# A batched matrix product with the second operand transposed: the first load in two transfers, one wait handed from TensorE to VectorE, the closing waits handed from GpSimd to SyncE

## The chip, the cores and the metric

The kernel runs on one core of a Trainium2 chip. The metric is the device time of one execution in microseconds (us); lower is better. The profile is one execution taken by the hardware profiler. Engines are named as there: PE is TensorE's matmul, PEld its weight load, DVE is VectorE, ACT is ScalarE, POOL is GpSimd, SP is SyncE; a "q" behind a name means the engine's sequencer. "L93" is line 93 of the kernel.

## The reference

```python
batch, m, k, n = 16, 512, 512, 512
a: (batch, m, k) float32      b: (batch, n, k) float32
return np.matmul(a, b.transpose(0, 2, 1)).astype(np.float32)
```

Sixteen products of 512x512 matrices are wanted, each of a with the transpose of b. The inputs are 2 x 16.8 MB, the output 16.8 MB.

## The kernel before

The 16 matrices are worked in 8 pairs. For each pair, u, one load brings two matrices of a (2 MB), another two matrices of b. All loads are issued by SP on one DMA queue. Each of the 128 partitions holds 8 rows of 512 float32 values, 16 KB in all; there are seven such load buffers, ld0 to ld6, and 16 loads, so that the eighth load waits until its buffer has been read. The first two loads (of a and b for the first pair) are cut into halves of 1 MB along the rows of a partition, lines L93 and L96, each half with a semaphore of its own: `s_ld` for the first, `s_second` for the second half.

DVE casts what has landed to bf16, in two halves (L116, L121), into `ha` and `hb`. PE transposes 128x128 blocks with an identity matrix (L185) into the PSUM tile `tp`; ACT copies the transposed a to `ta` (L137), DVE the transposed b to `tb` (L126). Then PE multiplies (L199, 32 matmuls of 128x512 per pair) into `ps`, and ACT copies each result to an output buffer (L153), of which there are seven, ob0 to ob6. An output of 1 MB is stored by one DMA. ACT issues the first (L163), SP the other 15 (L105).

Everything stands in one critical section, in which the engines are ordered by semaphores that are written out by hand, not by the framework. SP's order of loads and stores is written out as a string, `ORDER`, of 16 L and 15 S: seven loads, two of them in halves, are issued at the start without any wait; after these, loads and stores alternate by the string, each behind its own wait (a load for a free buffer, a store for a finished output). PE's work is a loop over the pairs on PE's sequencer (`Fori`, L172); the other engines' code is unrolled.

At the start POOL makes the identity `ident` in two steps (L67, L69), which raise `s_set` to 2. PE waits for that in front of its loop (L171). The wait in the loop's first step is `take(s_c, 1)`, for DVE's cast of the whole of `ha`.

At the end the last seven stores must have landed. A second critical section holds seven waits on POOL for this, one for each store semaphore (L212 to L214). Between the two sections the framework puts a meeting of the engines (L40): SP signals, every other engine answers, SP signals again. After the second section it puts a closing barrier over all engines (L240). SP stands in this closing part and waits for POOL to leave its section.

A wait on an engine is, in the built program, an instruction of the engine's sequencer, or is joined to the one that follows. In the trace POOL's seven waits, joined with those of the framework, are six instructions in a row.

Of the kernel before, what the change touches and what calls it, by code (L numbers as in the profile page):

```python
# [10 lines left out]
def kernel(  # L11
# [6 lines left out]
    nc = tc.nc  # L18
    P = 128
    batch, M, K = a.shape  # L20
    _, N, _ = b.shape
    J = M // P
# [5 lines left out]
    NL = 7  # L28
    NO = 7
# [4 lines left out]
    def sbuf(name, shape, dtype):  # L34
        return ctx.enter_context(nc.sbuf_tensor(name, shape, dtype))

    def sem(name):
        return tc.alloc_semaphore(name)

    with tc.tile_critical(no_gpsimd_drain=True):  # L40
        ident = sbuf("ident", [P, P], bf16)
        ld = [sbuf(f"ld{i}", [P, 2 * J, K], f32) for i in range(NL)]
# [8 lines left out]
        s_set = sem("s_set")  # L51
        s_ld = [sem(f"s_ld{i}") for i in range(NL)]
        s_second = [sem(f"s_second{i}") for i in range(2)]
        s_st = [sem(f"s_st{i}") for i in range(NO)]
# [23 lines left out]
        n_ld, n_st = 0, 1  # L78
        for what in ORDER:
            if what == "L":  # L80
                u, slot = n_ld // 2, n_ld % NL
                src = (a if n_ld % 2 == 0 else b)[2 * u:2 * u + 2].rearrange(
                    "e (p j) k -> (e p) j k", j=2 * J
                )
                if n_ld >= NL:

                    v = (n_ld - NL) // 2
                    if (n_ld - NL) % 2 == 0:
                        nc.sync.wait_ge(s_half, 2 * v + 2)
                    else:  # L90
                        nc.sync.wait_ge(s_tb, KO * v + 1)
                if n_ld < 2:
                    nc.sync.dma_start(  # L93
                        ld[slot][:, :J, :], src[:, :J, :]
                    ).then_inc(s_ld[slot], 16)
                    nc.sync.dma_start(  # L96
                        ld[slot][:, J:, :], src[:, J:, :]
                    ).then_inc(s_second[slot], 16)
                else:
                    nc.sync.dma_start(ld[slot][:], src).then_inc(s_ld[slot], 16)  # L100
                n_ld += 1
            else:
                slot = n_st % NO
                nc.sync.wait_ge(s_out, n_st + 1)
                nc.sync.dma_start(  # L105
                    out[n_st].rearrange("(p j) n -> p j n", j=J), ob[slot][:]
                ).then_inc(s_st[slot], 16)
                n_st += 1

        for u in range(pairs):
            for x, (h, s_c) in enumerate(((ha, s_ca), (hb, s_cb))):
                n = 2 * u + x
                nc.vector.wait_ge(s_ld[n % NL], 16 * (n // NL + 1))
                nc.vector.tensor_copy(  # L116
                    out=h[:, :J, :], in_=ld[n % NL][:, :J, :]
                ).then_inc(s_half, 1)
                if n < 2:
                    nc.vector.wait_ge(s_second[n], 16)  # L120
                nc.vector.tensor_copy(  # L121
                    out=h[:, J:, :], in_=ld[n % NL][:, J:, :]
                ).then_inc(s_c, 1)
            for ko in range(KO):
                nc.vector.wait_ge(s_tb, KO * u + ko + 1)
                nc.vector.tensor_copy(  # L126
                    out=tb[:, ko, :],
                    in_=tp[:, (2 * ko + 1) % 4].rearrange("k j p -> k (j p)"),
                ).then_inc(s_eb, 1)
# [38 lines left out]
        def take(s, n):  # L168
            nc.tensor.wait_ge(s, n).then_inc(s, -n)  # L169

        nc.tensor.wait_ge(s_set, 2)  # L171
        with nc.Fori(  # L172
            0, pairs, engines=[nc.tensor.engine], head_slot={nc.tensor.engine: 24}
        ):
# [33 lines left out]
                    t.then_inc(s_mm, 1)  # L208

    with tc.tile_critical(no_gpsimd_drain=True):  # L212
        for n in range(batch - NO, batch):
            nc.gpsimd.wait_ge(s_st[n % NO], 16 * (n // NO + 1))  # L214


# [28 lines left out]
```

## Time and profile before

| | us |
|---|---|
| median of 4 runs | 127.39 |
| lowest and highest run | 127.12 and 127.88 |
| the profiled execution, its whole time | 127.28 |
| span of the profile, first to last instruction | 125.5 |
| busy: PE, PEld | 89.7, 56.5 |
| busy: ACT, DVE, POOL | 70.7, 59.2, 0.7 |
| first load issued | 0.94 |
| first cast (L116) starts | 6.12 |
| first transposes (L185) start on PE | 11.08 |
| last matmul ends, last copy of ACT (L153) starts | 115.16, 115.19 |
| last store issued | 115.80 |

The whole time is 1.78 us longer than the span; that part lies before the first and after the last instruction of the profile. A DMA's time is not that of its issue: an issue on SP takes 0.33 to 0.75 us of SP's time, and the data land later, by 16 DMA engines that the transfer is spread over. A landing is the moment at which one of these engines raises the transfer's semaphore, so a transfer of this kernel has 16 landings, and the last one releases who waits. The page's busy shares are averages over the span; the DMA row and the GB/s row in its slices say what the DMA engines do at the same time.

### The profile page before, as it was taken

What the parts mean: (1) busy time and instruction counts of PE and PEld (TensorE: products, weight loads), DVE (VectorE), ACT (ScalarE), POOL (GpSimd) and SP (SyncE); (2) the same over time, 40 slices, a digit from 0 to 9 for tenths busy, and PEclk for the clock granted to TensorE, in tenths of its full rate; (3) what the DMA queues carried; (4) which work ended last, traced back from release to release, by engine and by line L of the source; (5) the groups of instructions that cost most, each with busy time, mean ns of one, the idle gap of its engine ahead of it and who ended that gap; (6) DMA issues with size and microseconds to landing.
All of it is one profiled execution on the core that took longest, in us unless ns stands there. A gap on an engine that the chain in (4) does not pass through costs nothing. (4 is left out here: it accounts for less than half of the span.)

```text
span 125.5 us, 1959 instructions
## 1 busy us (share of the span) xinstructions
PE 89.7 (71%) x768; PEld 56.5 (45%) x768; DVE 59.2 (47%) x64; ACT 70.7 (56%) x129; POOL 0.7 (1%) x6
## 2 busy tenths in 40 slices
PE   0003089799699969996999699879586999697000
PEld 0002088347544854494459346734383449342000
DVE  0035525962793386549906970780666476200000
ACT  4001226468946875795669467946755679566000
POOL 2000000000000000000000000000000000000000
PEclk9999999999999999999999999999999999999965
DMA  4999999999999999999999999999999999999960
GB/s 86 394 426 436 428 444 433 423 418 410 389 428 415 444 399 428 441 433 428 410 439 423 413 460 402 405 441 389 462 428 423 413 423 433 420 423 426 439 269 8
DMA packets 4899, 50.37 MB, mean 401 GB/s; under 512 B 544, under 2 KB 544, under 8 KB 544
## 3 DMA queue, kind: packets, MB, share of 16 engines
q1 hardware_dynamic: 4752, 49.29, 93.8%
q10 hardware_dynamic: 144, 1.05, 2.0%
q8 instruction: 1, 0.02, 0.0%
q14 instruction: 2, 0.02, 0.0%
HBM read 33.55 MB, written 16.78 MB: 401 GB/s over the span
## 5 line engine op out<-in xcount | busy, mean ns | idle before, releaser
L199 PE MATMUL ps<-tb,ta 128*128 128x512 bf16 x256 | 56.5, 379 | 8.4 <-PEq L169 8.4
L153 ACT COPY ob<-ps 128x512 f32<-128x512 f32 x64 | 37.5, 586 | 26.4 <-PE ps L199 26.4
L137 ACT COPY ta<-tp 128x512 bf16<-128x512 bf16 x64 | 32.6, 625 | 17.8 <-PE tp L185 17.8
L199 PEld LDWEIGHTS ps<-tb,ta 128*128 128x128 bf16 x256 | 24.4, 97 | 37.9 <-issue 9.5
L126 DVE COPY tb<-tp 128x1024 bf16<-128x1024 bf16 x32 | 22.1, 691 | 28.4 <-PE tp L185 28.4
L185 PE MATMUL tp<-ident,ha 128*128 128x128 bf16 x256 | 21.2, 230 | 11.1 <-PEq L169 11.1
L185 PE MATMUL tp<-ident,hb 128*128 128x128 bf16 x256 | 20.8, 228 | 6.0 <-PEq L169 6.0
L185 PEld LDWEIGHTS tp<-ident,ha 128*128 128x128 bf16 x256 | 17.1, 104 | 13.7 <-issue 11.1
L185 PEld LDWEIGHTS tp<-ident,hb 128*128 128x128 bf16 x256 | 16.7, 102 | 6.5 <-issue 6.5
L116 DVE CAST hb<-ld 128x2048 bf16<-128x2048 f32 x8 | 9.8, 1224 | 9.7 <-DMA ld<-in_b_dram 9.7
L116 DVE CAST ha<-ld 128x2048 bf16<-128x2048 f32 x8 | 9.8, 1219 | 6.9 <-DMA ld<-in_a_dram 6.9
L121 DVE CAST ha<-ld 128x2048 bf16<-128x2048 f32 x8 | 9.8, 1221 | 2.4 <-DMA ld<-in_a_dram 2.4
L121 DVE CAST hb<-ld 128x2048 bf16<-128x2048 f32 x8 | 9.8, 1221 | 1.3 <-DMA ld<-in_b_dram 1.3
L137 ACT ACT_TABLE_LOAD x1 | 1.3, 1283 | 0.9 <-SPq L40 0.9
L69 POOL TENSOR_SCALAR_AFFINE_SELECT ident<-ident 128x128 bf16<-128x128 bf16 x1 | 0.3, 292 | 0.2 <-POOL ident L67 0.2
L67 POOL MEMSET ident<- 128x128 bf16 x1 | 0.2, 204 | 0.5 <-SPq L40 0.5
L229 POOL MEMSET const-bfloat16-1.0<- 128x1 bf16 x1 | 0.1, 101 | 0.0
L229 POOL MEMSET const-uint8-127<- 128x1 uint8 x1 | 0.1, 101 | 0.0
L229 POOL MEMSET const-float32-0.0<- 128x1 f32 x1 | 0.1, 98 | 0.2 <-issue 0.2
L229 POOL MEMSET const-float32-1.0<- 128x1 f32 x1 | 0.1, 98 | 0.0
## 6 DMA issues: line engine op xcount, KB each, us to landing
out_dram<-ob SPq DMA_DIRECT2D x15, 1024.0 KB, 25.6
ld<-in_a_dram SPq DMA_DIRECT2D x7, 2048.0 KB, 30.3
ld<-in_b_dram SPq DMA_DIRECT2D x7, 2048.0 KB, 31.5
ld<-in_a_dram SPq DMA_DIRECT2D x2, 1024.0 KB, 6.7
ld<-in_b_dram SPq DMA_DIRECT2D x2, 1024.0 KB, 11.3
out_dram<-ob ACTq DMA_DIRECT2D x1, 1024.0 KB, 12.6
```

The costliest lines, as they stand in the source:

```text
L67: nc.gpsimd.memset(ident[:], 0.0).then_inc(s_set, 1)
L69: nc.gpsimd.affine_select(out=ident[:], in_=ident[:], compare_op=mybir.AluOpType.not_equal, fill=1.0, base=0, pattern=[[-1, P]], channel_m ...
L116: nc.vector.tensor_copy(out=h[:, :J, :], in_=ld[n % NL][:, :J, :]).then_inc(s_half, 1)
L121: nc.vector.tensor_copy(out=h[:, J:, :], in_=ld[n % NL][:, J:, :]).then_inc(s_c, 1)
L126: nc.vector.tensor_copy(out=tb[:, ko, :], in_=tp[:, (2 * ko + 1) % 4].rearrange("k j p -> k (j p)"),).then_inc(s_eb, 1)
L137: c = nc.scalar.copy(out=ta[:, ko, e * J * P:(e + 1) * J * P].rearrange("k (j p h) -> k j p h", j=J, h=2), in_=tp[:, (2 * ko) % 4, :, e * ...
L153: c = nc.scalar.copy(out=ob[i % NO][:, j, :].rearrange("m (p j) -> m p j", j=2 * J), in_=ps[:, j, :].rearrange("m (j p) -> m p j", j=2 * J),)
L185: t = nc.tensor.transpose(tp[:, (2 * ko + x) % 4, j, :], h[:, j, ko * P:(ko + 1) * P], ident[:],)
L199: t = nc.tensor.matmul(ps[:, j, :], ta[:, ko, (e * J + j) * P:(e * J + j + 1) * P], tb[:, ko, :].rearrange("k (j p) -> k j p", j=2 * J)[:, ...
L229: nc = _bacc.Bacc("TRN2", target_bir_lowering=False, num_devices=1)
```

## The change

Four things change.

- The first half of the first load is issued as two transfers, of partitions 0 to 31 and of partitions 32 to 127, onto the same semaphore. DVE's waits on that semaphore count 16 more from there on. The halves behind it are issued as before, one place later.
- PE no longer waits for the identity in front of its loop.
- DVE waits for it instead, before its first cast. PE's first work waits for that cast.
- SP waits, at the end of the first section, for six of the last seven stores. The second section holds one wait, on SP, for the last store; POOL has none there.

The arithmetic and all other transfers stay.

```diff
-                if n_ld < 2:
+                if n_ld == 0:
+                    for p in (slice(0, 32), slice(32, P)):
+                        nc.sync.dma_start(
+                            ld[slot][p, :J, :], src[p, :J, :]
+                        ).then_inc(s_ld[slot], 16)
+                elif n_ld == 1:
                     nc.sync.dma_start(
                         ld[slot][:, :J, :], src[:, :J, :]
                     ).then_inc(s_ld[slot], 16)
+                if n_ld < 2:
                     nc.sync.dma_start(
                         ld[slot][:, J:, :], src[:, J:, :]
                     ).then_inc(s_second[slot], 16)
...
+        for n in range(batch - NO, batch - 1):
+            nc.sync.wait_ge(s_st[n % NO], 16 * (n // NO + 1))
...
+        nc.vector.wait_ge(s_set, 2)
         for u in range(pairs):
             for x, (h, s_c) in enumerate(((ha, s_ca), (hb, s_cb))):
                 n = 2 * u + x
-                nc.vector.wait_ge(s_ld[n % NL], 16 * (n // NL + 1))
+                nc.vector.wait_ge(
+                    s_ld[n % NL], 16 * (n // NL + 1 + (1 if n % NL == 0 else 0))
+                )
...
-        nc.tensor.wait_ge(s_set, 2)
         with nc.Fori(
...
     with tc.tile_critical(no_gpsimd_drain=True):
-        for n in range(batch - NO, batch):
-            nc.gpsimd.wait_ge(s_st[n % NO], 16 * (n // NO + 1))
+        nc.sync.wait_ge(s_st[(batch - 1) % NO], 16 * ((batch - 1) // NO + 1))
```

In the built program the order of the work on PE, DVE and ACT is the same as before. SP issues one transfer more, and POOL's instructions after the identity are those of the meeting and of the closing barrier alone.

## The prediction

> **What bounds the kernel now.** I read the page's slices first, then the queues, then the windows in stretches of 10 us, then the start and the end. The slices say that the DMA engines never rest between start and end, and the queue line says that one queue does it:
>
> ```profile
> DMA  4999999999999999999999999999999999999960
> GB/s 86 394 426 436 428 444 433 423 418 410 389 428 415 444 399 428 441 433 428 410 439 423 413 460 402 405 441 389 462 428 423 413 423 433 420 423 426 439 269 8
> ...
> q1 hardware_dynamic: 4752, 49.29, 93.8%
> ```
>
> The windows (columns: stretch, its length, busy time of PE, PEld, DVE, ACT, POOL, granted clock, DMA share, GB/s) say it per stretch:
>
> ```profile
> 0.00:10.00 10.00, 0.00 (x0) 0.00 (x0) 1.52 (x2) 1.28 (x1) 0.70 (x6) 1.00 0.80 309
> 10.00:20.00 10.00, 4.96 (x46) 4.75 (x47) 4.77 (x5) 2.48 (x5) 0.00 (x0) 1.00 1.02 437
> 50.00:60.00 10.00, 8.94 (x89) 5.90 (x88) 6.61 (x8) 7.39 (x14) 0.00 (x0) 1.00 1.01 433
> 110.00:120.00 10.00, 5.15 (x24) 2.15 (x22) 0.00 (x0) 4.09 (x7) 0.00 (x0) 1.00 1.01 425
> 120.00:125.50 5.50, 0.00 (x0) 0.00 (x0) 0.00 (x0) 0.00 (x0) 0.00 (x0) 0.51 0.24 103
> ```
>
> The reader is to see three parts: a start of about 3 us in which DMA is not yet full, some 117 us at a share of 0.99 to 1.02 and about 425 GB/s, and an end of about 4 us in which it drains and the program closes. In the middle part no engine's work can set the time: whatever PE, DVE or ACT do sooner, the 50.37 MB are the same, and they pass at the same rate. The page's chain (PE, then ACT's last copy at 115.19 us) ends at the last store's issue and does not show the transfer behind it. So only two things can move the end: when the DMA stream starts and how evenly its 16 engines fill, and what follows the last landing.
>
> **The end.** The last store is issued at 115.80 us; its sixteenth and last landing is at 123.67 us, the one before it on that semaphore at 123.18, the third last at 122.50. The store before lands last at 121.24, 2.43 us earlier. The waits of SP and the closing lines between 123 and 126 us:
>
> ```profile
> SPq L240 <- POOLq L212: 8.0, 1, 8.0
> ...
> L240 POOLq EVENT_SEMAPHORE  x9: 17/43/43, 123.8 to 125.4; - x9
> L240 SPq EVENT_SEMAPHORE  x3: 17/17/7918, 116.6 to 125.4; - x3
> L240 SPq DRAIN  x3: 7/7/7, 124.5 to 124.9; - x3
> ...
> L240 POOLq COMPARE_BRANCH  x1: 33/33/33, 124.2 to 124.2; - x1
> ```
>
> POOL starts its released wait at 123.695, then walks through five more waits of 43 ns, 87 ns apart (123.79 to 124.13), branches at 124.22, raises its semaphore at 124.37, passes on at 124.46, and SP, which waited 7.92 us for this, is through at 124.51 and drains at 124.55 and 124.61 before the closing barrier. From landing to SP's first drain: 124.55 - 123.67 = 0.88 us.
>
> After the change SP does this itself. Six of the seven stores are waited for in the first section, the latest at 121.24; then the section's own close (SP L40 from 116.17 to 116.59 now, 0.42 us) runs from about 121.3 to 121.8. The last wait comes at 123.67, so 1.9 us of cover remain; the cover is the last store's own 2.43 us, and if it were gone the 0.42 us would stand on the path. On SP, after the landing: wake 0.03, the wait 0.03 (SP's L40 waits are 28 ns), branch to the next instruction 0.15 (SP's at the start: branch 0.789, DMA 0.942; POOL's above is also 0.15), raise 0.08 (L40, 116.174 to 116.252), drain to the next 0.13 (116.252 to 116.382), pass on and drain 0.05. Sum 0.47 us against 0.88: **-0.41 us**. The barrier after it (125.50 - 124.61) is the same code. SP's waits queue nothing else behind them: every load and store has been issued. The other four engines sit at SP's section close until 121.7 instead of 116.3; nobody needs them before 123.7. Since each price has its row, I give this 0.1 us either way.
>
> **PE's wait and DVE's wait.** PE leaves out a wait that ends at 1.71 us; it jumps at 1.80 and then stands until 11.08 for the first cast, so it gains about 0.7 us of waiting: 0. DVE takes over the wait; the identity is done at 1.67, and DVE's first cast starts at 6.12 when its data land. 4.4 us of cover, cost 0.
>
> **The first load in two.** It adds one issue on SP, of 0.38 to 0.43 us (L93, L96), and moves the eight loads behind it by that. They are covered. The closest is L96's first, which would be issued at about 1.81 and have its rows ready 1.02 later (as the first: issued 0.94, first packet 1.96), at 2.83; the engines come to it when they have finished the first, from 4.88 on. Behind it an issue takes 0.4 to 0.7 us and a transfer 2.5 us of the stream, so the cover grows. Bytes and the number of 8 KB rows are the same; 16 completion packets of 9 ns come on top, one per engine. What can change is the filling:
>
> ```profile
> 1.50:2.00 0.50, 0.00 (x0) 0.00 (x0) 0.00 (x0) 0.50 (x1) 0.17 (x1) 1.00 0.38 66
> 2.00:2.25 0.25, 0.00 (x0) 0.00 (x0) 0.00 (x0) 0.18 (x1) 0.00 (x0) 1.00 1.41 229
> 2.25:2.50 0.25, 0.00 (x0) 0.00 (x0) 0.00 (x0) 0.00 (x0) 0.00 (x0) 1.00 0.37 66
> 2.50:2.75 0.25, 0.00 (x0) 0.00 (x0) 0.00 (x0) 0.00 (x0) 0.00 (x0) 1.00 0.64 164
> 2.75:3.00 0.25, 0.00 (x0) 0.00 (x0) 0.00 (x0) 0.00 (x0) 0.00 (x0) 1.00 0.91 295
> ```
>
> From 1.96 to 3.00 these rows move 33 + 57 + 17 + 41 + 74 = 222 KB, where 425 GB/s would move 442: 0.52 us of the stream are missing. The 16 engines start their first packet between 1.96 and 2.84, on average at 2.21, and that packet takes 0.31 to 1.09 us, on average 0.70 instead of 0.31. If the rows are handed out one after the other, 32 rows reach all 16 engines early and the spread of starts shrinks. Bounds: at best the whole 0.52 is recovered, and the first packet comes 0.29 earlier (three quarters of the issue's 0.38): -0.81. At worst the second transfer pays the slow first packet again: +0.39 (0.70 - 0.31). Engines do not run dry between the two: two packets of 309 ns from 1.96 reach to 2.58, and the second issue, at about 1.38, brings rows 1.02 later, at 2.40. I take **-0.25**, the mean spread of starts (2.21 - 1.96), the nearest row.
>
> [...] The trace's row: transfers of 1.05 MB behind one another land 2.47 and 2.50 us apart (9.69, 12.16, 14.66), which is about 420 GB/s with no fixed part. [...]
>
> **Sum.** The profiled execution took 127.28 us, of which the span is 125.50. 127.28 - 0.41 - 0.25 = 126.62. Its time is 0.11 below the median of the runs, 127.39, from which the same sum gives 126.73. Forecast: **126.7**.
>
> **Rivals.**
>
> *The split does nothing.* The slow first packets, not the hand-out, make the gap; what speaks for it is that 11 of 16 engines start within 0.25 us already. Then only the end is left: 127.39 - 0.41 = 126.98, so 127.0.
>
> *PE's earlier jump moves a code transfer out of the stream.* In the window 5.9 to 6.9 us stands
>
> ```profile
> q8 instruction: 1, 0.02, 5.8%
> ```
>
> one packet of 16 KB at 5.96 us that took 0.93 us; the row behind it on that engine took 0.81 instead of 0.31. One engine is then 1.14 us behind the rest (the second transfer's last two landings are 8.55 and 9.69). If this is PE's code, and a jump at 1.1 instead of 1.8 brings it ahead of the first row at 1.96, that engine gains up to 1.4. The end gains only up to the next engine, 123.67 - 123.18 = 0.49: 126.73 - 0.49 = 126.2. Against it: from jump to packet it is 4.17 us now, so that by this row it would come at 5.3, still in the stream. [...]
>
> *The 32 rows lie on few engines (slower).* If they go as eight rows to four engines, as 128 rows go to sixteen, and the other 96 to all, those four have 14 packets where the rest have 6. That is 6 more than the even share of 8: 6 x 0.309 = 1.85 us later on them. It decides as soon as one of the four has less slack than that: landings of the last store run from 120.65 to 123.67, so only engines more than 1.85 before the end absorb it. At worst 126.73 + 1.85 = 128.6, slower than before. Against it: every transfer of the trace, loads and stores, has 16 landings; no transfer of 32 rows is in it.
>
> **How the numbers follow.** A measurement of this kernel tells a difference of about 0.5% from none: 0.64 us, so faster means under 126.75. The forecast's case gets 0.42, of which its scatter (the runs before lie from 127.12 to 127.88) puts 0.25 under that and 0.17 over. The split does nothing: 0.28, 0.07 under, 0.21 same. The code transfer moves: 0.20, 0.18 under, 0.02 same. Few engines: 0.10, 0.08 slower, 0.02 same. Sums: faster 0.50, same 0.42, slower 0.08. Range: from 126.0 (code transfer gone and a little more of the start than 0.25) to 127.4 (the second slow packet, 127.39 - 0.41 + 0.39 = 127.37); the slower rival stays outside.
>
> **What would show it.** The end: the last landing of the last store to the span's end is 1.83 us now, and should be about 1.4, with SP and not POOL ending it. The start: first packets still at about 1.96 or earlier, over 300 KB moved by 3.00 us. PE: first transposes not before the first cast; whatever they do, the DMA share stays at 1.00. The code packet: its time, and whether the first L96 transfer's last landing still trails by 1.1. The 32-row transfer: its number of landings. I would be wrong if the DMA engines' own pace, not the start, differs: 1% of 117 us is more than both terms together, and nothing in the change should cause it.

## The result and the profile after

The changed kernel takes 127.72 us (median of 35 runs, 127.28 to 128.90); the kernel before 127.34 (56 runs). The ratio is 1.0032, 95% interval 1.0019 to 1.0046: it is slower by 0.41 us (0.24 to 0.59), where 0.66 less was forecast (0.41 and 0.25), and outside the range of 126.0 to 127.4. The profiled execution took 127.95 us with a span of 126.2.

The page of the kernel after, its DMA rows over 40 slices of 3.15 us:

```profile
DMA  4999999999999999999999999999999999999980
GB/s 112 252 348 429 429 431 447 426 431 418 413 436 429 444 421 431 423 431 436 410 442 395 408 434 413 382 444 413 444 431 416 423 426 423 431 423 426 434 340 23
```

The DMA engines are busy as before, but in the second and third slice they move 252 and 348 GB/s, where it was 394 and 426. Busy and slow is what to see here: the share of busy time (the upper row) does not tell the two apart. From the fourth slice on the pace is that of before; between 20 and 120 us it is 425 GB/s, and was 423.

The windows of the kernel after, and under them those of the kernel before (stretch, length, five engines, clock, DMA share, GB/s):

```profile
2.00:3.00 1.00, 0.00 (x0) 0.00 (x0) 0.00 (x0) 0.19 (x1) 0.00 (x0) 1.00 1.10 295
3.00:5.00 2.00, 0.00 (x0) 0.00 (x0) 0.00 (x0) 0.00 (x0) 0.00 (x0) 1.00 0.99 258
5.00:7.00 2.00, 0.00 (x0) 0.00 (x0) 0.00 (x0) 0.00 (x0) 0.00 (x0) 1.00 1.02 246
7.00:9.00 2.00, 0.00 (x0) 0.00 (x0) 0.06 (x1) 0.00 (x0) 0.00 (x0) 1.00 0.96 360
```

```profile
2.00:3.00 1.00, 0.00 (x0) 0.00 (x0) 0.00 (x0) 0.18 (x1) 0.00 (x0) 1.00 0.83 188
3.00:5.00 2.00, 0.00 (x0) 0.00 (x0) 0.00 (x0) 0.00 (x0) 0.00 (x0) 1.00 0.94 365
5.00:7.00 2.00, 0.00 (x0) 0.00 (x0) 0.88 (x1) 0.00 (x0) 0.00 (x0) 1.00 1.08 442
7.00:9.00 2.00, 0.00 (x0) 0.00 (x0) 0.34 (x1) 0.00 (x0) 0.00 (x0) 1.00 0.96 406
```

From 2 to 3 us the changed kernel is ahead, 295 GB/s against 188, which is 107 KB. In the half microsecond before it is behind, 16 GB/s against the 66 that the prediction shows, which is 25 KB:

```profile
1.50:2.00 0.50, 0.00 (x0) 0.00 (x0) 0.00 (x0) 0.50 (x1) 0.17 (x1) 1.00 0.08 16
```

So by 3 us 82 KB are gained, or 0.19 us at 425 GB/s: the first packets of the 16 engines now start between 1.98 and 2.30 us, instead of 1.96 to 2.84. From 3 to 7 us it falls behind: 2 x (365 + 442 - 258 - 246) = 606 KB less, 1.4 us at 425 GB/s. An 8 KB packet takes 0.50 (3 to 5 us) and 0.54 us (5 to 7 us) there, on average, and 0.34 and 0.31 before. The second half-load (L102) lands its last part at 11.07 us instead of 9.69, the last store at 124.86 instead of 123.67.

The end, in the waits of SP and the closing lines of the kernel after:

```profile
SPq L116 <- DMA out_dram<-ob: 3.8, 2, 2.4
SPq L248 <- DMA out_dram<-ob: 1.7, 1, 1.7
```

```profile
L248 SPq EVENT_SEMAPHORE  x5: 17/27/1707, 123.1 to 126.1; - x5
...
L248 SPq DRAIN  x3: 7/7/7, 125.3 to 125.6; - x3
...
L248 SPq COMPARE_BRANCH  x1: 33/33/33, 124.9 to 124.9; - x1
```

SP reaches its last wait at 123.18 us and stands there 1.71 us, released by the DMA itself, where it stood 7.9 us for POOL; it branches at 124.92 and comes to the first drain of the closing barrier at 125.28. From the last landing to the end of the span there are 1.32 us (126.18 - 124.86) and were 1.83. So one part of the change pays 0.5 us at the end, and another costs more than that at the start.

### The profile page after: what moved, and what is told of

It is laid out like the page before. It is cut to its first block, busy times and chain, and to the rows that moved or that the text cites. A ratio compares the mean times of both kernels' runs of the same rounds, so it can differ in the third digit from the quotient of the medians.

```text
span 126.2 us, 1961 instructions
## 1 busy us (share of the span) xinstructions
PE 90.6 (72%) x768; PEld 57.6 (46%) x768; DVE 59.4 (47%) x64; ACT 70.7 (56%) x129; POOL 0.7 (1%) x6
## 5 line engine op out<-in xcount | busy, mean ns | idle before, releaser
L195 PE MATMUL tp<-ident,ha 128*128 128x128 bf16 x256 | 21.7, 233 | 12.5 <-PEq L180 12.5
L195 PE MATMUL tp<-ident,hb 128*128 128x128 bf16 x256 | 21.4, 232 | 6.1 <-PEq L180 6.1
L195 PEld LDWEIGHTS tp<-ident,hb 128*128 128x128 bf16 x256 | 17.3, 105 | 6.5 <-issue 6.5
```

The lines of the kernel that those rows point to most:

```text
L195: t = nc.tensor.transpose(tp[:, (2 * ko + x) % 4, j, :], h[:, j, ko * P:(ko + 1) * P], ident[:],)
```

## The experiments

**Each part alone, and the rest without the cut.** Theories: the cut by partitions slows the packets ("partition theory"), or PE's earlier jump does, by its code packet ("jump theory").

`e1_split`, the first-load part of the change alone:

```diff
+                if n_ld == 0:
+                    for p in (slice(0, 32), slice(32, P)):
+                        nc.sync.dma_start(
+                            ld[slot][p, :J, :], src[p, :J, :]
+                        ).then_inc(s_ld[slot], 16)
...
```

> The kernel before with the first load in 32 and 96 partitions alone. Partition theory (the cut by partitions slows the packets of the start: 0.5 us each instead of 0.31 between 3 and 7 us): the slow packets are here too, the last landing of the first half-load is past 8 us instead of 6.09, time +0.8 us against before (after is +0.38 with an end of -0.44). Jump theory (PE's early jump puts its 16 KB code packet at 3.17 us and that slows the start): no slow packets, 6.1 us, time -0.25 to 0 us.

Measured: ratio to before 1.0067 (1.0046 to 1.0088), +0.85 us. Its windows:

```profile
2.00:3.00 1.00, 0.00 (x0) 0.00 (x0) 0.00 (x0) 0.19 (x1) 0.00 (x0) 1.00 0.91 254
3.00:5.00 2.00, 0.00 (x0) 0.00 (x0) 0.00 (x0) 0.00 (x0) 0.00 (x0) 1.00 1.04 279
5.00:7.00 2.00, 0.00 (x0) 0.00 (x0) 0.00 (x0) 0.00 (x0) 0.00 (x0) 1.00 0.97 274
```

The slow packets are here without the jump (0.49 and 0.45 us on average in the two last rows). The first half-load is complete at 7.15 us, not past 8; that point of the expectation was too late. The profiled execution is the fastest of the 12 (127.31 us; their median is 128.08), and its last store lands at 123.70 us, as before (123.67), although its second half-load is 1.2 us late. So what is lost at the start does not reach the end in every execution; the 0.85 us rest on the median of the runs, not on this trace.

`e2_end`, the closing waits alone:

```diff
+        for n in range(batch - NO, batch - 1):
+            nc.sync.wait_ge(s_st[n % NO], 16 * (n // NO + 1))
...
-        for n in range(batch - NO, batch):
-            nc.gpsimd.wait_ge(s_st[n % NO], 16 * (n // NO + 1))
+        nc.sync.wait_ge(s_st[(batch - 1) % NO], 16 * ((batch - 1) // NO + 1))
```

> The kernel before with the closing waits on SP alone. Both theories: from the last landing to the end of the span 1.39 us instead of 1.83, time -0.41 us, 0.9968 of before. A rival would be that SP's earlier waiting delays something at the end: then 0.

Measured: 0.9963 (0.9939 to 0.9987), -0.47 us; from the last landing to the end of the span 1.32 us, where 1.39 was expected.

`e3_pe`, the wait for the identity moved, alone:

```diff
+        nc.vector.wait_ge(s_set, 2)
...
-        nc.tensor.wait_ge(s_set, 2)
```

> The kernel before with PE's wait for the identity given to DVE alone. Partition theory: 0, within 0.1 us; the code packet may move from 5.96 us to 3 or so, the bulk of the packets stay at 0.31 us. Jump theory: slow packets of 0.5 us from 3 to 7 us, time +0.8 us.

Measured: 0.9991 (0.9965 to 1.0017). The 16 KB code packet comes at 3.69 us instead of 5.96 and still takes 0.93; the packets are those of before:

```profile
3.00:5.00 2.00, 0.00 (x0) 0.00 (x0) 0.00 (x0) 0.00 (x0) 0.00 (x0) 1.00 1.00 381
5.00:7.00 2.00, 0.00 (x0) 0.00 (x0) 0.00 (x0) 0.00 (x0) 0.00 (x0) 1.00 1.02 426
```

`e4_end_pe`, the diffs of `e2_end` and `e3_pe` together:

> The changed kernel without the cut of the first load. Partition theory: -0.41 us against before, 126.9, and so 0.8 us under the changed kernel. Jump theory: the loss stays, +0.4 us against before.

Measured: 0.9953 (0.9931 to 0.9975), 126.74 us. It beats both kernels. Its windows, the measure for the kernels below:

```profile
3.00:5.00 2.00, 0.00 (x0) 0.00 (x0) 0.00 (x0) 0.00 (x0) 0.00 (x0) 1.00 0.99 381
5.00:7.00 2.00, 0.00 (x0) 0.00 (x0) 0.00 (x0) 0.00 (x0) 0.00 (x0) 1.00 1.01 422
```

The jump theory falls; the cut is the loss, 1.0 us between this kernel and the changed one (1.0032 / 0.9953 = 1.0079).

**Why the cut is slow.** Three theories: a part of the partitions is reached over a part of SBUF's places ("place theory", a supposition of the author's: no trace shows the places); any second transfer costs that much ("count theory"); a narrow stretch of HBM is read slowly ("source theory"). The place theory counts in row times, one being the 0.309 us of an 8 KB packet: all 128 partitions take 8; that 32 take 4 and the 96 behind them 8 is the author's estimate from `e1_split`, whose second half-load is 1.2 us late (4 x 0.309 = 1.24). All the following kernels are `e4_end_pe` with another cut, unless said otherwise.

`e5_64_64`:

```diff
+                    for p in (slice(0, 64), slice(64, P)):
```

> As e4_end_pe (end and PE's wait changed), but the first half-load goes as two transfers of partitions 0 to 63 and 64 to 127. Place theory: a transfer to a part of the partitions can be written only at a part of SBUF's places, so 0 to 31 and then 32 to 127 took 4 + 8 row times where 128 take 8 (4 x 0.309 = 1.24 us more; the second half-load of e1_split landed 1.2 us later). Here each transfer has half the places with 8 rows each: 8 + 8, so 8 x 0.309 = 2.47 us more than e4_end_pe, packets of 0.6 us until about 8 us. Count theory (a second transfer costs 1.2 us whatever it holds, the rows being small shares per engine): 1.2 us more.

`e13_64_64_reads`:

```diff
+                    for p in ((slice(0, 64), slice(0, P, 2)), (slice(64, P), slice(1, P, 2))):
+                        nc.sync.dma_start(
+                            ld[slot][p[0], :J, :], src[p[1], :J, :]
+                        ).then_inc(s_ld[slot], 16)
```

> As e5_64_64, but the first transfer reads every second of the 128 source rows and the second one the others, so that both spread over the whole 2 MB of the source; the rows of a thus lie in other partitions, and the first pair's products have their rows in another order. Place theory (SBUF's partitions decide): the same as e5_64_64, 2.47 us more than e4_end_pe. Source theory (a narrow stretch of HBM is slow to read, 64 rows lying within 1 MB): 0 to 0.3 us more than e4_end_pe.

`e12_rows_2_2` (`e6_by_rows` has `slice(0, 1), slice(1, J)`):

```diff
+                    for p in (slice(0, 2), slice(2, J)):
+                        nc.sync.dma_start(
+                            ld[slot][:, p, :], src[:, p, :]
+                        ).then_inc(s_ld[slot], 16)
```

> As e4_end_pe, but the first half-load goes as two transfers of all 128 partitions, two of the four rows each: pieces of 4 KB instead of 8, same bytes per transfer as e5_64_64. Place theory: no slow packets, first landings at about 4 us, time as e4_end_pe within 0.3 us. Count theory: 1.2 us more than e4_end_pe.

> As e4_end_pe, but the first half-load goes as two transfers of all 128 partitions, of one row and of three rows: the quarter and three quarters of the changed kernel, cut the other way (pieces of 2 KB and of 6 KB). Place theory: no slow packets of 0.5 us from 3 to 7 us, time as e4_end_pe within 0.3 us. Count theory: 1.2 us more than e4_end_pe.

Measured: `e5_64_64` 128.45 us, ratio to before 1.0096 (1.0068 to 1.0125); `e13_64_64_reads` 128.70, 1.0106 (1.0059 to 1.0153); `e12_rows_2_2` 126.62, 0.9972 (0.9944 to 0.9999); `e6_by_rows` 126.68, 0.9958 (0.9928 to 0.9987). Two transfers of half a load each cost 1.8 us more when they are cut by partitions than when they are cut by rows (128.45 - 126.62). So it is not the count. Spreading the reads changes nothing, so it is not the source (the product of `e13_64_64_reads` has its rows in another order; it serves for the time alone). The windows of `e5_64_64`, then of `e13_64_64_reads`, `e12_rows_2_2` and `e6_by_rows`:

```profile
3.00:5.00 2.00, 0.00 (x0) 0.00 (x0) 0.00 (x0) 0.00 (x0) 0.00 (x0) 1.00 1.02 242
5.00:7.00 2.00, 0.00 (x0) 0.00 (x0) 0.00 (x0) 0.00 (x0) 0.00 (x0) 1.00 1.04 225
```

```profile
3.00:5.00 2.00, 0.00 (x0) 0.00 (x0) 0.00 (x0) 0.00 (x0) 0.00 (x0) 1.00 1.02 258
5.00:7.00 2.00, 0.00 (x0) 0.00 (x0) 0.00 (x0) 0.00 (x0) 0.00 (x0) 1.00 1.04 225
```

```profile
3.00:5.00 2.00, 0.00 (x0) 0.00 (x0) 0.00 (x0) 0.00 (x0) 0.00 (x0) 1.00 0.88 289
5.00:7.00 2.00, 0.00 (x0) 0.00 (x0) 0.00 (x0) 0.00 (x0) 0.00 (x0) 1.00 1.05 434
```

```profile
3.00:5.00 2.00, 0.00 (x0) 0.00 (x0) 0.00 (x0) 0.00 (x0) 0.00 (x0) 1.00 0.99 349
5.00:7.00 2.00, 0.00 (x0) 0.00 (x0) 0.00 (x0) 0.00 (x0) 0.00 (x0) 1.00 0.99 395
```

225 GB/s is about half of the 425 of the steady stream, which is what the place theory supposes of 64 partitions. The place theory had asked for 2.47 us; the time shows 1.8, while the second half-load lands 2.4 to 2.5 us later in its bulk (10.42 to 11.05 us against 7.91 to 8.68), 0.3 of it from a later first packet. Why less of this shows in the time stays open. The last engine is later by 1.7 only (11.24 against 9.53), which would fit. But in the two kernels that follow the order is the other way round: against `e4_end_pe` the last engine is later by 2.2 (`e14_middle`) and 1.7 us (`e15_lower`), the time by 1.6 and 2.2, with intervals that overlap. The cut by rows brings the first landings forward, to 3.1 us in `e6_by_rows`, and gains nothing that can be measured over `e4_end_pe`.

**The same sizes at other partitions.** Does the number of the partitions decide, or which they are?

```diff
+                    for p in (slice(32, 96), slice(0, 32), slice(96, P)):    # e14_middle
+                    for p in (slice(0, 64), slice(64, 96), slice(96, P)):    # e15_lower
...
```

DVE's wait on that semaphore counts 32 more in both, for three transfers.

> As e4_end_pe, but the first half-load goes as three transfers, of partitions 32 to 95, then 0 to 31, then 96 to 127. [...] Theory that any transfer of fewer than 128 partitions is slow in the ratio of its partitions: 64 of 128 and 32 of 128 cost the same in both kernels, no difference between e14 and e15.

> As e14_middle with the same sizes in the same order, but of partitions 0 to 63, then 64 to 95, then 96 to 127. [...] Theory that only the number of partitions counts: the same as e14_middle.

Measured: 128.42 us, 1.0080 (1.0050 to 1.0109), and 129.02, 1.0123 (1.0065 to 1.0181). The stretch in which both are at work on their first 64 partitions, `e14_middle` and then `e15_lower`:

```profile
3.50:4.20 0.70, 0.00 (x0) 0.00 (x0) 0.00 (x0) 0.00 (x0) 0.00 (x0) 1.00 1.06 421
```

```profile
3.50:4.20 0.70, 0.00 (x0) 0.00 (x0) 0.00 (x0) 0.00 (x0) 0.00 (x0) 1.00 1.02 257
```

64 partitions each, and one goes at 421, the other at 257 GB/s. By packets it is plainer still. Each engine has four of this transfer. The third and the fourth take 0.31 us on 15 of 16 engines in `e14_middle`; in `e15_lower` their medians are 0.61 and 0.63. And `e14_middle` reads its 64 rows from one narrow stretch of the source, at full pace: a second case against the source theory. The number of partitions does not decide, which partitions does. Why 0 to 63 are slow and 32 to 95 are not, no run shows.

The total is less clear. An estimate from the runs above: 4 row times for 32 to 95 (four packets an engine, at the 0.31 us of the third and fourth in `e14_middle`), 8 for 0 to 63 (0.61 and 0.63 us a packet in `e15_lower`), and 4 for each 32, as estimated from `e1_split`. That makes 12 for `e14_middle` and 16 for `e15_lower` against 8, so 1.24 and 2.47 us more than `e4_end_pe`. `e15_lower`'s second half-load lands 2.8 us behind that of `e4_end_pe` (medians of the landings), from a stream that starts 0.3 later; that fits. `e14_middle`'s is 2.5 us behind, from a start 0.4 later; that does not fit, and the two kernels' intervals overlap. In `e14_middle` packets of 0.6 to 0.8 us go on until 8 us, past the two transfers of 32. The packets of the other cuts lag too: in the changed kernel, `e5_64_64` and `e15_lower` an engine's second packet still takes 0.31 to 0.36 us (medians), the third 0.52 to 0.61, and slow ones go on behind the cut transfers. So, `e14_middle` apart, the row times give about the sum, and not which packet pays. The reason stays open.

**The cut twice.** `e9_both_first` is the changed kernel with both first half-loads cut, a's and b's; DVE's wait on each counts 16 more.

```diff
-                if n_ld == 0:
+                if n_ld < 2:
...
```

> The changed kernel with the cut at 32 on both first half-loads, of a and of b, instead of a's alone. Place theory: the loss of the cut twice. The changed kernel is 1.0 us over e4_end_pe, so 2.0 us over it here, 128.7; slow packets again from about 9.5 to 13 us. Theory that only the cold start of the stream makes the cut costly: the second cut costs nothing, as the changed kernel, 127.7.

Measured: 131.80 us, 1.0341 (1.0260 to 1.0422), 5.0 us over `e4_end_pe` (1.0341 / 0.9953 = 1.0390). The theory of the cold start falls: the second cut, at 9 to 15 us in a full stream, slows it again, in the windows of `e9_both_first`:

```profile
7.00:9.00 2.00, 0.00 (x0) 0.00 (x0) 0.00 (x0) 0.00 (x0) 0.00 (x0) 1.00 1.00 373
9.00:12.00 3.00, 0.00 (x0) 0.00 (x0) 1.23 (x1) 0.00 (x0) 0.00 (x0) 1.00 1.03 238
12.00:15.00 3.00, 0.00 (x0) 0.00 (x0) 0.61 (x1) 0.00 (x0) 0.00 (x0) 1.00 1.00 235
```

But it costs 3.9 us (1.0341 / 1.0032 = 1.0308) and not 1. Two parts of that are seen: the bulk of the second cut load falls 2.3 us further behind (4.0 behind `e4_end_pe` by the median landing, 1.7 at the load before), and one engine is then 2.9 us behind the rest (18.52 against 15.59 us), where it is 0.9 in the changed kernel at that place. The count of row times does not give either; this stays open.

## Why the prediction was wrong

*The bound.* Right that the DMA stream sets the time: its engines stay busy throughout, and in the profiled execution the second half-load is 1.5 us late (9.64 against 8.13 us, medians of the landings) and the last store 1.19. But "only two things can move the end" left out a third, the pace of the packets while the engines are busy. The prediction names it as its sign of being wrong, "the DMA engines' own pace", and holds that nothing in the change should cause it; the cut did, from 3 to 7 us. The check that it set, a share of 1.00, was met (0.99 and 1.02) and told nothing.

*The end, -0.41 us.* Right. It measured -0.47 (`e2_end`); in the traces of before and after, landing to SP's first drain of the closing barrier went from 0.88 to 0.42 us, where 0.47 was summed up. The cover was as said: SP is at its last wait at 123.18 us, 1.7 us early.

*PE's and DVE's wait, 0.* Right: 0.9991, within its interval. DVE's first cast comes at 8.94 us for its data, with the identity done at 1.67 us.

*The first load in two, -0.25 us.* This step failed, in sign and beyond its own bounds (-0.81 to +0.39): alone it measures +0.85. What it said of the first microsecond happened: the spread of first packets shrank from 0.88 to 0.33 us, and 0.19 us were gained by 3 us. What it missed is in its own sentence "Bytes and the number of 8 KB rows are the same": it took the duration of a packet, 309 ns, from rows in which every transfer covers all 128 partitions, and carried it to transfers that do not (0.50 and 0.54 us on average from 3 to 7 us). The bounds were drawn from the first packet's slowness and never let the following packets be slow. By the author's count of row times, itself drawn from `e1_split`, the cut costs (4 + 8 - 8) x 0.309 = 1.24 us; the second half-load, by the medians of its landings, is 1.2 us late in `e1_split` against before (9.29 and 8.13 us) and 1.6 us in the changed kernel against `e4_end_pe` (9.64 and 8.03).

*No fixed part per transfer.* Right, as read from the landings 2.47 and 2.50 us apart: the cuts by rows issue one transfer more and pay nothing (126.62 and 126.68 us, against 126.74 without a cut).

*The rival "few engines".* It saw that 32 rows may be spread unevenly, and looked at the wrong end of the transfer. Each of the two transfers still has 16 landings, and the first packets start on 16 engines, so all engines take part. With the reads spread out the time is the same (128.70 and 128.45 us), and 64 partitions run at 421 or 257 GB/s by which they are: that is the uneven side. Its price, 1.85, was not paid.

*The rival "code transfer".* Half right. The packet follows PE's jump: 3.2 us in the changed kernel, 3.7 in `e3_pe` and 3.6 in `e4_end_pe`, against 5.96 before and 6.03 and 5.95 in `e1_split` and `e2_end`, where PE still waits. The 4.17 us from jump to packet, which the prediction carried over, are no fixed time: 2.0 us in the changed kernel, 2.5 in `e3_pe` and `e4_end_pe`. In all these it stays in the stream, and no gain shows. In the four kernels that begin with 64 partitions it comes at 2.16 to 2.17 us, ahead of the first load packet; in three of them the last landing of the second half-load then trails the one before by 0.1 to 0.2 us, where it is 0.85 in `e4_end_pe`. So a part of the rival's gain may lie hidden in those kernels' losses; no run here shows it alone. That it is PE's code is the author's reading of these times; the traces name its queue (`q8 instruction`), not its engine.

Sum of the parts alone: +0.85 - 0.47 - 0.11 = +0.27 us; the whole measures +0.41 (0.24 to 0.59).

## What to carry to other kernels

When the DMA stream is the bound, cut a load along what lies within a partition, not along the partitions: here the same bytes in as many transfers cost nothing one way and 1.8 us the other. A packet's duration holds for the transfers it was read from (0.31 us here, 0.50 and 0.54 behind the cut); before carrying it to another shape, ask which engines send it and which partitions they write: 64 partitions ran at 421 or at 257 GB/s, by which 64 they were. In a stream that is always busy, read GB/s beside the share (1.02 stood beside 246 GB/s, 1.01 beside 425), and test parts apart: here a gain of 0.5 us was hidden under a loss of 0.85.

## What the runs showed of the hardware that was not expected

- An issue on SP of the first load took 0.38 to 0.39 us for 128 and for 32 partitions, but 0.55 to 0.61 us for 64, and the first packet came at 2.28 to 2.36 us instead of 1.97. So the stream of these four kernels starts 0.3 to 0.4 us later. The reason stays open.
- The code packet of 16 KB holds one DMA engine for 0.93 to 1.39 us. Where it comes among the loads, the last landing of the second half-load trails the one before by 0.85 to 1.34 us in seven of nine kernels (0.4 in `e6_by_rows`, 3.4 in `e9_both_first`). That the time follows that engine is not shown.
- A second cut load behind the first cost four times as much as the first alone, 3.9 us and 1.0 (`e9_both_first`).
